# A hybrid decoder layer on one core: dense work in pinned pieces, modulation sums in an earlier stage, four borders reordered

## The chip, the cores and the metric

The kernel runs on one core of a Trainium2 chip. The metric is the device time of one execution in microseconds, the median of several; three runs of the kernel before gave 2275.9 to 2278.8, median 2276.56. TensorE (PE) multiplies, VectorE (DVE) and ScalarE (ACT) work elementwise and read the matmul banks (PSUM), GpSimd (POOL) does small powers and issues stores, SyncE (SP) issues loads. Each of them executes its queue in order.

## The reference

One layer of a post-norm decoder, sequence and width 1024, float32. It is a mixing part and a squared-ReLU MLP, each with modulation sums from a condition vector:

```python
mod = silu(c) @ w_ada + b_ada            # 6 sections of 1024: shift, scale, gate, twice
u = x * (1 + scale1) + shift1
hq, hf, hi, hg, rq, rk, rv, rg, ga, gb = split(u @ w_in)
ya = hgrn2(hq, hf, hi, hg) @ w_pa        # 8 heads of a gated linear recurrence
yb = retention(rq, rk, rv, rg, positions) @ w_pb     # 4 heads, rotary, chunks of 128
y = (sigmoid(ga) * ya + sigmoid(gb) * yb) @ w_o
x = layer_norm(alpha * x + (1 + gate1) * y)
u = x * (1 + scale2) + shift2
y = square(relu(u @ w_up + b_up)) @ w_down + b_down
out = layer_norm(alpha * x + (1 + gate2) * y)
```

HGRN: S_t = diag(f_t) S_{t-1} + k_t v_t, o_t = S_t^T q_t with k = 1 - f. Retention is the same with a fixed decay per head.

## The kernel before

**Dense products.** A float32 number is kept as a high part and a rest (`split`, L169: a copy on ACT to the high part, then a subtraction on DVE for the rest), and a product is three matmuls (`mm3`, L175 to L177) of 128x128 by 128x512. `dense_T` (L362) makes one 128x512 block with 24 of them. Larger products use a seven-product scheme (`natural`, `seven`). Weights come through one stream: pieces of 512 KB are loaded by SP into a ring of four buffers ("raw"), split, and handed out by `W` in a fixed order, some tiles ahead.

**Stages.** (1) Start: the first two modulation sections, u, its splits. (2) Input projection by `natural` (hi, rv; the rotary angles are computed beside it) and `seven` (24 "kept" groups: hg, ga, then rq, rg, rk, rg for each retention head); results go to DRAM. (3) HGRN: for each head four dense halves (q and forget gate, `h_dense`) are woven with the recurrence `h_rec` of the head before (`weave`, 4 steps against 13). (4) Retention: 4 heads of 10 steps (`r_head`: two steps of transposes and scores, eight chunks), with the HGRN branch's projection (`h_merge`, w_pa) and the 16 remaining groups of modulation sums (`ada_group`) dealt among them. (5) `merge_seven` (w_pb), (6) `out_proj` with the first norm and u for the MLP, (7) up by `seven`, (8) `down_seven` with the last norm.

**The recurrence of a head** (`h_rec`) on PE: L793 (scores inside pairs), then three levels of L831 (scores of ever larger blocks), L863 (k transposed), L874 (state updates), L890 and L894 (output), and a few steps later L917 (output transposed, in `h_out`). Between two levels DVE copies scores under masks (L799, L800, L840) and multiplies k and X by decays (L807, L821, L822, L848 to L851), which the next level reads. ACT makes sigmoids (L752 to L759), copies banks (L865, L897) and scales outputs (L903) by factors from POOL (L911).

**Retention.** `r_qk` transposes k (L1048), splits it, and `r_scores` (L1061) needs one of the two "a" banks that the split has to free. Each chunk updates the state bank G (L1113, copied by ACT at L1115) and makes an output bank (mm3 into psb, L1121, copied at L1123). `r_norm` and, four steps later, `r_out` (L1145, L1147) follow.

**What sets the order.** The program is traced in Python order; a planner then fixes each engine's queue. It works by its own estimate of when an instruction is ready, takes what is traced earlier first, and may put later work ahead of work that it takes to be waiting. `keep_in_program_order` puts an instruction behind all that was traced before it on its engine (a pin; it bounds it on one side only), `issue_after` does so for a block of instructions behind a given one, and `behind` orders two matmuls of one bank. `later(n, f)` defers f by n ticks of the recurrence.

**The modulation sums.** A group sums w_ada columns weighted by the condition: eight DVE steps of 128x256 (`ada_step`, L563 and L565), then a matmul with ones (`ada_row`, L1164, or `ada_cols`, L571), the bias, and a store or a column of `mod`. Groups of sections gate2, gate1, scale2, shift2, four each.

**Borders.** At the border to retention, `h_merge` first splits eight tiles of 128x1024 (the HGRN heads' output, loaded through the raw ring, "ohr") in one step. In `out_proj` each row of 128 is normalized one step before its transposes (L1413, in `out_second`); the last row's come after the last matmul of the stage. In `down_seven`, five products are prepared (`prepare`: splits of h and w_down) before the first is multiplied, while the last additions of `seven` (L431) are still to come.

Of the kernel before, what the change touches and what calls it, by code (L numbers as in the profile page):

```python
# [19 lines left out]
P = 128  # L20
# [34 lines left out]

PA_STEPS = [6 + (31 * i + 7) // 15 for i in range(16)]

ADA_STEPS = [4 + (32 * i + 7) // 15 for i in range(16)]
# [66 lines left out]
class Trunk:  # L125
# [43 lines left out]
    def split(self, hi, lo, src):  # L169
        self.nc.scalar.activation(hi, src, AF.Copy)  # L170
        self.nc.vector.tensor_tensor(lo, src, hi.bitcast(F32), op=ALU.subtract)  # L171
# [196 lines left out]


# [52 lines left out]
    def seven(self, groups):  # L422
# [4 lines left out]
        for g, (key, use) in enumerate(groups):  # L427

            def put(m, half, bank, kept):
                t = self.et()  # L430
                V.tensor_tensor(t, bank, kept, op=ALU.add)  # L431
                use(m, half, t, False)
# [127 lines left out]
    def ada_step(self, acc, w, k, first):  # L560
        sc = self.cond[:, k:k + 1]
        if first:
            self.nc.vector.tensor_scalar(acc, w, sc, None, op0=ALU.mult)  # L563
        else:
            self.nc.vector.scalar_tensor_tensor(acc, w, sc, acc, op0=ALU.mult, op1=ALU.add)  # L565
# [172 lines left out]
    def h_cols(self, p, what, hd):  # L738
# [9 lines left out]
        for hf in (0, 1):  # L748
            sl = slice(hf * 512, hf * 512 + 512)
            pd = self.dense_T(wh, wl, hf)  # L750
# [6 lines left out]
            else:  # L757
# [3 lines left out]
                nc.vector.tensor_tensor(s["q"][:, 0:2, hf * 256:hf * 256 + 256], pr, sr, op=ALU.mult)  # L761
# [8 lines left out]
    def h_rec(self, p, hd):  # L770
# [18 lines left out]
        for bk in range(4):  # L789
            pa = ps[bk].rearrange("p (c w b) -> p c w b", c=2, w=3)  # L790
            for c in (0, 1):
                n = 2 * bk + c
                nc.tensor.matmul(pa[:, c], k[:, n * P:(n + 1) * P], q[:, :, n * 64:(n + 1) * 64], start=True, stop=True)  # L793
# [19 lines left out]
        for ln, sz in enumerate(H_SIZES):  # L813
# [13 lines left out]
            for bk in range(4):  # L827
                for c in (0, 1):
                    n = 2 * bk + c
                    mv = X[:, :, n * P:(n + 1) * P].rearrange("p w (b r) -> p b w r", r=4 * sz)[:, :, :, sz:]  # L830
                    nc.tensor.matmul(ps[bk][:, c * 192:(c + 1) * 192].rearrange("p (b w r) -> p b w r", w=2, r=3 * sz),  # L831
                                     k[:, n * P:(n + 1) * P], mv, start=True, stop=True)
# [26 lines left out]
        for hf, tag in ((0, "b"), (1, "a")):  # L859
            pb = self.ps(tag)  # L860
            for c in range(4):
                cs = slice(hf * 512 + c * P, hf * 512 + c * P + P)
                nc.tensor.transpose(pb[:, c * P:(c + 1) * P], k[:, cs], self.ident)  # L863
# [7 lines left out]
        for hf, tag in ((0, "a"), (1, "c")):  # L871
            pu = self.ps(tag)
            for c in range(4 - hf):
                nc.tensor.matmul(pu[:, c * P:(c + 1) * P], kt[hf][:, c * P:(c + 1) * P], vn(4 * hf + c), start=True, stop=True)  # L874
# [10 lines left out]
        for hf, tag in ((0, "c"), (1, "a")):  # L885
            po = self.ps(tag)
            prev = None
            for c in range(4):
                n = 4 * hf + c
                r = l = nc.tensor.matmul(po[:, c * P:(c + 1) * P], S[hf][:, c, :], vn(n), start=True, stop=n == 0)  # L890
                if prev is not None:
                    self.behind(r, prev)
                if n > 0:
# [39 lines left out]
    def gate_proj(self, what, dst, ms):  # L933
        nc = self.nc
        for m in ms:
            wh, wl = self.W((what, m // 2, m % 2))
            for hf in (0, 1):
                pd = self.dense_T(wh, wl, hf)
# [7 lines left out]
    def h_merge(self):  # L946
        nc = self.nc
        o = []
        for e in range(KT):
# [3 lines left out]
            self.split(o[e][:, 0], o[e][:, 1], t)  # L953
        yield
# [13 lines left out]
    def rotary(self):  # L968
# [30 lines left out]
        for s in range(T // W):  # L999
            cs = slice(s * W, (s + 1) * W)  # L1000
            pi = self.rp.tile([P, W], I32, tag="rot_i", bufs=1, name=self.uid("rot"))
            nc.sync.dma_start(pi, self.i["positions"][0:1, cs].to_broadcast([P, W]))
            a, m, y, n = (self.rp.tile([P, W], F32, tag="rot_" + c, bufs=1, name=self.uid("rot")) for c in "amyn")
# [828 lines left out]
```

## Time and profile before

| | |
|---|---|
| median of 3 runs | 2276.56 us |
| profiled execution, its time | 2276.54 us |
| profiled execution, its span | 2274.7 us |
| PE busy | 2216.5 us (97%) |
| DVE busy | 1661.5 us (73%) |
| ACT busy | 969.2 us (43%) |
| POOL busy | 289.1 us (13%) |
| HBM read, written | 275.87 MB, 97.53 MB |

The span runs from the first instruction to the last; the time has a little around it. A matmul's recorded duration overlaps the next one's, so busy time on PE is close to the sum of start-to-start distances where it runs without a break. In the views, a wait is shown with the instruction whose end released it, and "x" counts instructions.

### The profile page before, as it was taken

How to read it: one execution, taken by the hardware profiler on the slowest of the kernel's cores; microseconds unless marked ns; L12 is line 12 of the kernel's file. 1: busy time of each engine (PE TensorE's matmuls, PEld its weight loads, DVE VectorE, ACT ScalarE, POOL GpSimd, SP SyncE). 2: the span in 40 equal slices, each digit the busy share in tenths (PEclk: the TensorE clock that was granted, in tenths of full speed). 3: DMA queues.
4: the chain of work that ended last, by engine and by line, in shares of the span. 5: the costliest groups of instructions: out<-in, count | busy, mean ns of one | idle time of the engine just before them, and what ended most of it. 6: DMA issues, size and time to landing. Idle time of an engine off the chain costs nothing.

```text
span 2274.7 us, 29056 instructions
## 1 busy us (share of the span) xinstructions
PE 2216.5 (97%) x10214; PEld 1824.2 (80%) x10214; DVE 1661.5 (73%) x3024; ACT 969.2 (43%) x1627; POOL 289.1 (13%) x444
## 2 busy tenths in 40 slices
PE   6999999999999999999999999999999999999997
PEld 4888888888888888888867777888888888788886
DVE  7748776467676587887776777977796665667669
ACT  4533344433333323323353333452575555643441
POOL 0111011111111100100112222112011111100001
PEclk9999999999999999999999999999999999999999
DMA  9545633332333511222387878645344444967653
GB/s 306 188 159 171 195 127 118 110 109 103 118 105 115 168 47 48 75 72 77 130 278 247 267 243 286 228 153 192 111 148 153 153 153 153 315 227 245 204 175 130
DMA packets 228563, 375.33 MB, mean 165 GB/s; under 512 B 16584, under 2 KB 126912, under 8 KB 228160
## 3 DMA queue, kind: packets, MB, share of 16 engines
q1 hardware_dynamic: 199664, 279.66, 38.7%
q0 software_dynamic: 28432, 93.35, 11.0%
q8 instruction: 80, 1.31, 0.2%
q14 instruction: 67, 0.55, 0.1%
q10 hardware_dynamic: 320, 0.45, 0.1%
HBM read 275.87 MB, written 97.53 MB: 164 GB/s over the span
## 4 chain that ended last, share of the span: by engine, by line
PE 82%; DVE 8%; issue 5%; DMA 3%; ACT 2%; POOL 1%; SPq 0%; ACTq 0%; DVEq 0%; POOLq 0%
PE psd L175 14%; PE psd L176 14%; PE psd L177 14%; PE psa L176 5%; PE psa L177 5%; PE psa L175 5%; PE psc L175 4%; PE psc L177 4%; PE psc L176 4%; PE psb L1121 2%; PE psc L1113 2%; PE psb L175 2%; PE psb L176 2%; PE psb L177 1%; PE psa L831 1%
## 5 line engine op out<-in xcount | busy, mean ns | idle before, releaser
L175 PE MATMUL psd<-U,bh 128*128 128x512 f32 x616 | 239.8, 389 | 0.0
L176 PE MATMUL psd<-U,bh 128*128 128x512 f32 x616 | 239.6, 389 | 0.0
L177 PE MATMUL psd<-U,bl 128*128 128x512 f32 x616 | 239.5, 389 | 0.0
L170 ACT ACTIVATE bh<-s 128x512 fp32r<-128x512 f32 x204 | 128.9, 633 | 249.0 <-PE psd L176 82.0
L171 DVE TENSOR_TENSOR bl<-raw,bh 128x512 fp32r<-128x512 f32 x153 | 104.6, 691 | 144.5 <-ACT bh L170 143.9
L175 PE MATMUL psd<-U,wh 128*128 128x512 f32 x504 | 203.9, 407 | 0.3 <-ACT U L170 0.3
L176 PE MATMUL psd<-U,wh 128*128 128x512 f32 x504 | 198.9, 395 | 1.0 <-DVE U L171 0.7
L177 PE MATMUL psd<-U,wl 128*128 128x512 f32 x504 | 199.7, 396 | 0.0
L171 DVE TENSOR_TENSOR bl<-s,bh 128x512 fp32r<-128x512 f32 x204 | 140.1, 687 | 65.2 <-ACT bh L170 64.8
L170 ACT ACTIVATE bh<-raw 128x512 fp32r<-128x512 f32 x153 | 96.9, 637 | 194.6 <-PE psd L176 101.9
L170 ACT ACTIVATE U<-hr 128x512 fp32r<-128x512 f32 x112 | 70.6, 630 | 155.3 <-issue 64.2
L175 PEld LDWEIGHTS psd<-U,bh 128*128 128x128 f32 x616 | 115.7, 188 | 24.3 <-ACT e L419 0.3
L176 PEld LDWEIGHTS psd<-U,bh 128*128 128x128 f32 x616 | 115.7, 188 | 24.0
L177 PEld LDWEIGHTS psd<-U,bl 128*128 128x128 f32 x616 | 115.6, 188 | 23.9
L170 ACT ACTIVATE wh<-raw 128x512 fp32r<-128x512 f32 (+1 forms) x78 | 52.7, 693 | 185.8 <-PE psd L176 138.6
L175 PE MATMUL psa<-U,bh 128*128 128x512 f32 x312 | 121.4, 389 | 0.0
L176 PE MATMUL psa<-U,bh 128*128 128x512 f32 x312 | 121.4, 389 | 0.0
L177 PE MATMUL psa<-U,bl 128*128 128x512 f32 x312 | 121.4, 389 | 0.0
L176 PEld LDWEIGHTS psd<-U,wh 128*128 128x128 f32 x504 | 95.5, 189 | 20.0 <-DVE U L171 2.8
L175 PEld LDWEIGHTS psd<-U,wh 128*128 128x128 f32 x504 | 95.0, 190 | 19.9 <-issue 2.2
L177 PEld LDWEIGHTS psd<-U,wl 128*128 128x128 f32 x504 | 95.3, 189 | 19.3
L171 DVE TENSOR_TENSOR U<-hr,U 128x512 fp32r<-128x512 f32 x112 | 77.2, 689 | 43.8 <-ACT U L170 43.7
(448 smaller groups left out, 5641.2 us busy)
## 6 DMA issues: line engine op xcount, KB each, us to landing
raw<-in_w_in SPq DMA_DIRECT2D x126, 512.0 KB, 4.2
raw<-in_w_down SPq DMA_DIRECT2D x48, 512.0 KB, 4.4
raw<-in_w_pb SPq DMA_DIRECT2D x36, 512.0 KB, 4.8
raw<-in_w_ada SPq DMA_DIRECT2D x32, 512.0 KB, 5.2
raw<-in_w_up SPq DMA_DIRECT2D x32, 512.0 KB, 3.8
adw<-in_w_ada SPq DMA_DIRECT2D x16, 512.0 KB, 7.7
rv_d<-e POOLq DMA_DIRECT2D x32, 256.0 KB, 3.1
rg_d<-e POOLq DMA_DIRECT2D x32, 256.0 KB, 2.3
```

What stands on the lines that cost most here:

```text
L170: self.nc.scalar.activation(hi, src, AF.Copy)
L171: self.nc.vector.tensor_tensor(lo, src, hi.bitcast(F32), op=ALU.subtract)
L175: r = mm(out, wh, uh, start=start, stop=False, skip_group_check=more)
L176: mm(out, wh, ul, start=False, stop=False, skip_group_check=more)
L177: return r, mm(out, wl, uh, start=False, stop=stop, skip_group_check=more)
L831: nc.tensor.matmul(ps[bk][:, c * 192:(c + 1) * 192].rearrange("p (b w r) -> p b w r", w=2, r=3 * sz), k[:, n * P:(n + 1) * P], mv, start=T ...
L1113: mm(G[e], l[:, n % 2, es], r, start=n == 0 and i == 0, stop=i == 2, skip_group_check=n > 0)
L1121: mm(po, st["q"][:, e, n * P:(n + 1) * P], gs[e], start=False, stop=e == 1)
```

## The change

Five things are changed.

1. HGRN's dense halves and the later gb gates yield after every six matmuls (`pieces_T`), so that they are dealt out in pieces: `H_FILL` gives the number of pieces after each of a head's 13 steps, and the dense work runs four pieces (one half) further ahead than by whole heads (`H_LEAD`). The first matmul of each group of the recurrence, and the product of q and its sigmoid on DVE, are pinned. The remaining gate pieces fill the tail of the last head and the two score steps of the first retention head, six to one.
2. The 16 groups of modulation sums leave the retention stage and its weight ring and run in the input projection beside the kept groups that aren't rq or rk (`ada_rest`): 64 parts of 256 KB with two buffers of their own, the first of each part's two steps pinned, and the end of a group two parts later, on bank "b". The rotary steps now all lie beside `natural`, in a pool that is closed before the sums' pool opens.
3. Merge: `h_merge` splits two tiles per step, pinned on ACT and DVE, in retention steps 2 to 5.
4. Last row: half of the plain up product (its first 24 matmuls) is traced before the flush that makes the last row's transposes, which are pinned behind it; the "relu" tiles become four.
5. Down: the fourth and fifth preparation stand behind the last addition of `seven` on DVE (`issue_after`).

Beside these, "ot" in the retention stage has three buffers in place of two.

```diff
+H_FILL = (0, 4, 3, 0, 3, 0, 2, 0, 1, 0, 2, 0, 1)
+H_LEAD = 4
...
-    def split(self, hi, lo, src):
-        self.nc.scalar.activation(hi, src, AF.Copy)
-        self.nc.vector.tensor_tensor(lo, src, hi.bitcast(F32), op=ALU.subtract)
+    def split(self, hi, lo, src, pin=lambda r: r):
+        pin(self.nc.scalar.activation(hi, src, AF.Copy))
+        pin(self.nc.vector.tensor_tensor(lo, src, hi.bitcast(F32), op=ALU.subtract))
...
+    def pieces_T(self, wh, wl, half):
+        pd = self.ps("d")
+        for k in range(KT):
+            uh, ul = self.ublk(k, half)
+            self.mm3(pd, wh[:, k], wl[:, k], uh, ul, k == 0, k == KT - 1)
+            if k in (1, 3, 5):
+                yield
+        return pd
...
-                V.tensor_tensor(t, bank, kept, op=ALU.add)
+                self.last_sum = V.tensor_tensor(t, bank, kept, op=ALU.add)
...
-            pd = self.dense_T(wh, wl, hf)
+            pd = yield from self.pieces_T(wh, wl, hf)
...
-                nc.vector.tensor_tensor(s["q"][:, 0:2, hf * 256:hf * 256 + 256], pr, sr, op=ALU.mult)
+                self.tc.keep_in_program_order(
+                    nc.vector.tensor_tensor(s["q"][:, 0:2, hf * 256:hf * 256 + 256], pr, sr, op=ALU.mult))
...
-                nc.tensor.matmul(pa[:, c], k[:, n * P:(n + 1) * P], q[:, :, n * 64:(n + 1) * 64], start=True, stop=True)
+                r = nc.tensor.matmul(pa[:, c], k[:, n * P:(n + 1) * P], q[:, :, n * 64:(n + 1) * 64], start=True, stop=True)
+                if n == 0:
+                    self.tc.keep_in_program_order(r)
...
-            self.split(o[e][:, 0], o[e][:, 1], t)
-        yield
+            self.split(o[e][:, 0], o[e][:, 1], t, self.tc.keep_in_program_order)
+            if e % 2:
+                yield
...
-        ot = self.rt("ot", (P, 4, P), 2)
+        ot = self.rt("ot", (P, 4, P), 3)
...
+    def ada_rest(self):
+        ap = self.aw
+        parts = [(s, g, q) for s, g in ADA_ORDER for q in range(4)]
...
+        for n, (s, g, q) in enumerate(parts):
+            if q == 0:
+                acc = ap.tile([P, 256], F32, tag="adacc", bufs=2, name=self.uid("acc"))
+            w = loaded.pop(n)
+            for j in (0, 1):
+                r = self.ada_step(acc, w[:, j], 2 * q + j, q + j == 0)
+                if j == 0:
+                    self.tc.keep_in_program_order(r)
+            if n + 2 < len(parts):
+                load(n + 2)
+            if q == 1 and ends is not None:
+                ends()
...
-        self.tick(True)
-        drain(self.u2)
...
+                r = nc.tensor.transpose(pt[:, k * P:(k + 1) * P], z[:, (4 * q + k) * P:(4 * q + k + 1) * P], self.ident)
+                if t == 7 and k == 0:
+                    self.tc.keep_in_program_order(r)
...
-        for n in range(AHEAD):
+        for n in range(3):
             prepare(n)
+        with self.tc.issue_after(self.last_sum.ins):
+            for n in range(3, AHEAD):
+                prepare(n)
...
-            for _ in k.seven([(key, use) for key, _, use in kept]):
-                next(rotary, None)
+            k.aw = k.pool("ada", "left", se)
+            ada = k.ada_rest()
+            for n, _ in enumerate(k.seven([(key, use) for key, _, use in kept])):
+                if n // 3 < len(kept) and kept[n // 3][0][0] not in ("rq", "rk"):
+                    next(ada, None)
+                    if n % 3 == 2:
+                        next(ada, None)
+            drain(ada)
...
-        drain(k.h_dense(0))
         gb = k.gate_proj("gb", k.gb_d, range(4, KT))
+        fill = chain(*(k.h_dense(h) for h in range(HH)), gb)
+        for _ in range(16 + H_LEAD):
+            next(fill)
         for h in range(HH):
-            if h + 1 < HH:
-                weave(k.h_dense(h + 1), k.h_head_rec(h), 4, 13)
-            else:
-                weave((next(gb) for _ in range(4)), k.h_head_rec(h), 4, 18)
+            rec = k.h_head_rec(h)
+            for n in H_FILL:
+                next(rec)
+                for _ in range(n):
+                    next(fill)
+            for _ in rec:
+                next(fill)
...
-            weave(gb, (next(heads) for _ in (0, 1)), 4, 2)
-            next(merge)
+            weave(fill, (next(heads) for _ in (0, 1)), 6, 1)
             for n in range(2, 10 * RH):
+                if n < 6:
+                    next(merge)
                 next(heads)
-                if n in ADA_STEPS:
-                    k.ada_group(*ADA_ORDER[ADA_STEPS.index(n)])
...
             k.out_proj(first)
+            plain = k.up_plain()
+            next(plain)
+            k.tick(True)
+            drain(k.u2)
```

The same pin stands on the first matmul of each bank group in L831 (per level), L863, L874 and L890.

More of the change, by code (lines that the diff above doesn't have):

```diff
@@ L1145, in r_out, with load @@
             nc.tensor.transpose(pb[:, e * P:(e + 1) * P], of[:, e * P:(e + 1) * P], self.ident)
-        ot = self.rt("ot", (P, 4, P), 2)
+        ot = self.rt("ot", (P, 4, P), 3)
         nc.vector.tensor_tensor(ot, pb.rearrange("p (e t) -> p e t", e=4), rg, op=ALU.mult)
         nc.gpsimd.dma_start(self.or_d[h].rearrange("(e p) t -> p e t", p=P)[:, :, n * P:(n + 1) * P], ot)
-    def ada_group(self, sec, g):
-        raws = self.W(("ada", sec, g))
-        acc = self.rp.tile([P, 256], F32, tag="adacc", bufs=2, name=self.uid("acc"))
-        for k in range(KT):
-            self.ada_step(acc, raws[k // 4][:, k % 4, :], k, k == 0)
+    def ada_rest(self):
+        ap = self.aw
+        parts = [(s, g, q) for s, g in ADA_ORDER for q in range(4)]
+        loaded = {}
+        def load(n):
+            s, g, q = parts[n]
+            c0 = s * D + 256 * g
+            t = loaded[n] = ap.tile([P, 2, 256], F32, tag="adw", bufs=2, name=self.uid("adw"))
+            self.nc.sync.dma_start(t, self.i["w_ada"][256 * q:256 * q + 256, c0:c0 + 256].rearrange("(k p) c -> p k c", p=P))
+        load(0)
+        load(1)
+        yield
+        ends = None
+        for n, (s, g, q) in enumerate(parts):
[5 more added lines that the diff above has]
+                if j == 0:
+                    self.tc.keep_in_program_order(r)
+            if n + 2 < len(parts):
+                load(n + 2)
+            if q == 1 and ends is not None:
+                ends()
+            if q == 3:
+                ends = lambda acc=acc, s=s, g=g: self.ada_end(acc, s, g)
+            yield
+        ends()
@@ L1477, in up_plain @@
                 use(m, half, self.dense_T(*wt[m], half), True)
+                if (half, m) == (0, 0):
+                    yield
     def down_seven(self):
@@ L1718, in build @@
             k.sin = k.rp.tile([P, T], F32, name="sin")
-            rotary = k.rotary()
-            for n, _ in enumerate(chain(*(k.natural(key, put) for key, _, put in wide))):
-                if n >= 28 and n % 4 == 1:
-                    next(rotary)
-            for _ in k.seven([(key, use) for key, _, use in kept]):
-                next(rotary, None)
+            with ExitStack() as st:
+                k.rt_p = k.pool("rotparts", "left", st)
+                rotary = k.rotary()
+                for n, _ in enumerate(chain(*(k.natural(key, put) for key, _, put in wide))):
+                    if n >= 20 and n % 4 == 1:
+                        next(rotary)
+                drain(rotary)
+            k.aw = k.pool("ada", "left", se)
[6 more added lines that the diff above has]
+            drain(ada)
     k.hst = {}
```

50 lines of the change are left out of this document (25 added, 25 removed).

## The prediction

> **What bounds the kernel now.** I read the page first, then the waits of the TensorE queue, then the timeline around each long wait.
>
> ```profile
> core 0: 2274.7 us, clock 0.997
> ```
>
> ```profile
> PE 2216.5 (97%) x10214; PEld 1824.2 (80%) x10214; DVE 1661.5 (73%) x3024; ACT 969.2 (43%) x1627; POOL 289.1 (13%) x444
> ```
>
> TensorE (PE) bounds everything: of the span only 2274.7 - 2216.5 = 58 us pass without a matmul. No matmul is removed, so what can be won is idle time. The waits of PE between 780 and 1970 us:
>
> ```profile
> PE psa L831 <- DVE k L807: 10.4, 7, 1.8
> PE psa L1061 <- DVE U L171: 6.7, 3, 3.6
> PE psb L175 <- ACT U L1123: 2.4, 2, 1.2
> PE psd L175 <- DVE e L431: 2.1, 1, 2.1
> PE psa L1413 <- ACT z L1391: 2.0, 2, 1.1
> PE psc L1113 <- ACT g L1115: 0.8, 1, 0.8
> PE psa L831 <- DVE U L822: 0.7, 1, 0.7
> PE psa L1145 <- DVE ot L1147: 0.3, 1, 0.3
> PE psa L1048 <- DVE ot L1147: 0.3, 1, 0.3
> ```
>
> Columns: total, times, longest, in us. Together 25.7 us; the other 32 lie at the start and the end, which the diff doesn't touch. L831 waits once in each of the eight HGRN heads; L1061 (the retention scores) three times; L175, L1113, L1145 and L1048 sit in the retention stage; L1413 at the output projection (one of its two waits is the last row of the stage, 1.1); psd L175 at the start of down. These are the places that the diff names. One HGRN head, PE:
>
> ```profile
> 834.71 0.39 PE L176 MATMUL psd<-U,wh 128*128 128x512 f32 x1
> 834.94 0.39 PE L177 MATMUL psd<-U,wl 128*128 128x512 f32 x1
> 835.16 1.46 PE L793 MATMUL psa<-hq,k 128*128 128x192 f32 x8
> 836.46 1.46 PE L793 MATMUL psc<-hq,k 128*128 128x192 f32 x8
> 837.76 0.60 PE L917 MATMUL psb<-cst,ob 128*128 128x128 f32 x4
> ...
> 838.66 0.40 PE L177 MATMUL psd<-U,wl 128*128 128x512 f32 x1
> 840.67 1.57 PE L831 MATMUL psa<-U,k 128*128 128x192 f32 x8 [1.61 <-DVE k L807]
> ...
> 848.62 1.46 PE L831 MATMUL psa<-U,k 128*128 128x192 f32 x8
> ```
>
> A dense matmul is recorded with 0.39 but the next starts 0.227 later: 0.16 of each record overlaps the next, so a wait costs its idle time and 0.16 more. A record of L793 (and L831, same shape) takes 1.30/8 = 0.162; the four transposes of L917 0.44. Between L793 and the first L831 stand only three dense matmuls (the last at 838.66), and DVE is not done by then:
>
> ```profile
> 837.05 0.69 DVE L761 TENSOR_TENSOR hq<-psd,sg 128x512 f32<-128x512 f32 x1 [2.06 <-ACT sg L759]
> ...
> 839.89 0.72 DVE L807 TENSOR_TENSOR k<-k,f 128x512 f32<-128x512 f32 x1
> ```
>
> DVE stood 2.06 us in front of L761, a product of the next head that needs a sigmoid, with the work that L831 needs queued behind it.
>
> **HGRN in pieces.** Same matmuls; each 24-matmul half becomes four pieces of six (6 x 0.227 = 1.36 us), placed by H_FILL, and the first matmul of every recurrence group is pinned behind them. Four pieces (5.45 us) now lie between L793 and the first L831. From L793's end (837.76) to L807's end (840.61) DVE needed 2.85 us with the 2.06 stall, which is covered; L761 is pinned later on DVE. Removed: 11.1 us of waits and 8 x 0.16 = 1.3, so **12.4**.
>
> What is late next? The last product before the second and the third L831 group is L822 (durations, then first and last start):
>
> ```profile
> L822 DVE TENSOR_TENSOR U<-U,D x2: 681/687/693, 847.2 to 854.5; 128x512 f32<-128x512 f32 x2
> ```
>
> The second L831 group had 848.62 - 840.67 = 7.95 us from the first; now it has 16 x 0.162 + 0.44 + 18 x 0.227 = 7.12. The first L822 ends at 847.9, 7.2 after the first group began: late by 0.1, and by 0.6 more if L761, now pinned near there, goes ahead of it. The third has 2.6 + 4.09 = 6.68, and its L822 ended 855.2 - 848.62 = 6.6 after: no wait, 0.5 if a weight split falls in between. Then the transposes:
>
> ```profile
> 859.49 0.60 ACT L752 ACTIVATE f<-psd 128x512 f32<-128x512 f32 x1 [9.26 <-PE psd L177]
> ...
> 861.78 0.59 ACT L865 ACTIVATE kt<-psb 128x512 f32<-128x512 f32 x1
> ```
>
> Four gate activations (2.3 us) precede the copy L865. The new order ends a forget-gate half right before the transposes, so kt can be ready 0.2 + 2.3 + 0.6 = 3.1 us after it, while PE gets there after 0.87 + 1.36 = 2.2: up to 0.9 late, 0 if the planner (which may still pull unpinned dense matmuls ahead) fills it. New waits per head: 0 to 2.1. I take 0.3, near the lower end, since both L822 rows come out within 0.1 of enough: 2.4 in all. Net **-10.0** (0 to 2.1 x 8 = 17 against 12.4: from -12.4 to +4.4).
>
> **Modulation sums.** 16 groups of eight DVE steps leave the retention stage for the second half of the input stage (hg, ga and rg groups); 32 loads of 512 KB become 64 of 256 KB, no longer in the ring of four "raw" buffers.
>
> ```profile
> L565 DVE SCALAR_TENSOR_TENSOR acc<-raw,small,acc 128x256 f32<-128x256 f32 x112 | 52.6, 483 | 1.6
> ```
>
> ```profile
> 520.00:558.00 38.00, 38.00 (x170) 31.46 (x169) 27.89 (x45) 14.27 (x24) 4.33 (x8) 1.00 0.33 112
> ```
>
> The second row is a window of one rotated group (which gets no sums) and one rg: after its length PE, weight loads, DVE, ACT, POOL, clock, DMA share. DVE has 27.9 of 38 and gets 8 x 0.48 = 3.9: 84%. The DMA engines are a third busy. PE sits at 38.00 of 38.00; what hides the sums are the weight blocks split ahead of it. On SP the 64 loads stand in order among the w_in loads, and each waits until DVE has freed one of two buffers: behind a late one wait the next w_in pieces, and behind a pinned sum whose load is late wait the additions that free PE's banks. A group's four parts lie 19/4 = 4.8 us apart, so two loads ahead give 9 us for a landing (the 512 KB merge loads below took 6.3). I take 0, up to +3. The closing matmuls, eight bias rows on SP and eight small stores on POOL (4.3 of 38 busy) move along at the same cost; the two rotary steps that lay beside the first kept groups move back into the stage before, where PE doesn't wait either.
>
> The retention stage loses 16 x 8 x 0.48 = 61 us of DVE, but DVE load is not what made PE wait there:
>
> ```profile
> 1271.84 0.63 ACT L170 ACTIVATE wh<-raw 128x512 fp32r<-128x512 f32 x1 [5.48 <-DMA raw<-in_w_pa]
> ```
>
> ```profile
> 1273.85 2.05 PE L1061 MATMUL psa<-U,U 128*128 128x128 f32 x16 [2.85 <-DVE U L171]
> ```
>
> ACT stood 5.48 us on a weight split whose load had not landed, with the copy that the scores need behind it in order. Of the four raw buffers the sums held two at a time; without them w_pa is loaded a group ahead. So 2.85 goes, and likewise 2.4 (psb) and 0.6 ("ot" has three buffers now): with restarts 5.9 + 5 x 0.16 = 6.7; I take **-6.0** (-6.7 to -3).
>
> **Scores and merge.** The longest wait of L1061 is where the retention stage begins:
>
> ```profile
> 1144.44 2.05 PE L1061 MATMUL psa<-U,U 128*128 128x128 f32 x16 [3.64 <-DVE U L171]
> ```
>
> ```profile
> L170 ACT ACTIVATE U<-ohr x8: 1057/1060/1067, 1140.2 to 1152.6; 128x1024 fp32r<-128x1024 f32 x8
> L171 DVE TENSOR_TENSOR U<-ohr,U x8: 1216/1224/1226, 1141.3 to 1153.7; 128x1024 fp32r<-128x1024 f32 x8
> ```
>
> ```profile
> ohr<-oh_d SPq DMA_DIRECT2D x8, 512.0 KB, 6.3
> ```
>
> A third, 6.7 - 3.64 - 2.85 = 0.2, precedes it. The eight merge splits ran ahead of the second scores' splits. Now they are pinned behind and dealt two at a time over four retention steps, so 0.2 + 3.6 + 0.8 (L1113) and restarts, 5.2, go. But their work (8 x 1.06 ACT, 8 x 1.22 DVE) stands among those steps, and a slot of the ring turns over in 6.3 + 1.06 + 1.22 = 8.6 us; with w_pa prefetched into two of four slots, eight tiles take four rounds, 34 us. An ACT queue that waits on a landing holds the copies that the recurrence needs. New waits 0 to 10; I take 4: **-1.2** (-5.2 to +5).
>
> [...] The 16 matmuls behind the 3.64 us wait took 2.05, as did those behind 2.85: no restart price beyond 0.16. [...]
>
> **Last row and down.** The first 24 up matmuls (5.45 us) now precede the last row's transposes, which lacked 1.1: **-1.3** with the restart. Behind them one more dense group covers the splits that follow. At down, two of five preparations go behind the last sum on DVE:
>
> ```profile
> 1960.55 0.69 DVE L431 TENSOR_TENSOR e<-psd,e 128x512 f32<-128x512 f32 x1
> ```
>
> Four splits of 0.6 (pitch) earlier, this sum ends 2.4 earlier, more than the 2.1 wait; the two preparations are needed three products (8 us) later. **-2.0** (-2.2 to -1).
>
> Sum: -10.0 - 6.0 - 1.2 - 1.3 - 2.0 = -20.5. The profiled execution took 2276.54 (1.8 outside its span), like the median 2276.56: **2256.0 us**.
>
> **The rivals.** (1) Pinned transposes wait in HGRN. L917 now follows L793 after six dense matmuls:
>
> ```profile
> 869.64 0.59 ACT L897 ACTIVATE ob<-psc 128x512 f32<-128x512 f32 x1
> ...
> 875.43 2.45 ACT L903 ACTIVATE ob<-ob,rs 128x128 f32<-128x128 f32 x8 [3.01 <-POOL rs L911]
> ```
>
> From L897 to the first half's four L903 (875.43 + 1.3) is 7.1 us; PE gets there after what is left of the second output bank (16 records of 0.11, the pitch of a transpose, so 1.7, less some 0.6 before L897 starts), one piece and L793: 1.1 + 1.36 + 2.6 = 5.0. If the planner misjudges this by 2.1, as it misjudged L807 by 1.6, that is 8 x 2.1 = 17 instead of 2.4: 2270.5. Against: any of the 24 unpinned matmuls can go ahead.
> (2) The merge ring binds with 10 us: 2262.
> (3) Slower: the DVE chain between L831 groups becomes the bound. If L921, L761 and two weight splits (4 x 0.6 = 2.4) all fall inside it at both inner levels, each head waits 2 x 2.4 + 0.1 = 4.9, 39 in all, against 12.4 + 10.5 won: 2276.5 + 16 = 2293. It decides from 22.9/8 = 2.9 us per head. Against: the rows above have one L921 inside a level and still fit.
> (4) The change doesn't do what it says: the planner draws dense work off ahead of the pinned groups, so HGRN's waits only move (0), w_pa is helped by half (-3), the ring binds (+4.8): 0 - 3 + 4.8 - 1.3 - 2.0 = -1.5, 2275.
> [...]
>
> **Chances.** Forecast 0.60; (1) 0.14; (2) 0.12; (3) 0.07; (4) 0.07. About 0.2% (4.6 us) can be told from no change: faster is below 2272. Faster 0.60 + 0.12 + 0.10 of (1) = 0.82; same 0.04 + 0.07 = 0.11; slower 0.07. Low end: everything that can go, 12.4 + 6.7 + 5.2 + 1.3 + 2.2 = 27.8, is 2248.8; high end at (1) with some margin: 2249 to 2272.
>
> **What would show it.** Right: L831 <- L807 gone from the waits, under 3 us left in HGRN; no ACT wait of microseconds on w_pa; L1061 waiting under 2 us in all; no L1413 wait at the last row; no psd wait on L431; PE still at 38.00 of 38.00 beside the sums. Wrong: new PE waits named L831 <- L822 or U, L874 <- kt, L917 <- ob, or a retention wait on g (L1115) behind a landing of ohr.

## The result and the profile after

The kernel after takes **2257.3 us** (median of 5 runs, 2256.0 to 2258.9), the kernel before 2276.56 (5 runs, 2275.5 to 2278.8): ratio **0.9911, 95% interval 0.9900 to 0.9922**, 0.9% faster, where 2256.0 (2249 to 2272) was predicted. Its profiled execution has a span of 2256.5 us, 18.2 less than before. That the sum came out right doesn't mean that its terms did, and several of them didn't.

Line numbers move in the kernel after: mm3 is L177 to L179 (before L175 to L177), the splits L172 and L173, the HGRN scores L805 and L845 (L793, L831) with the products in front of them L821, L835 and L836 (L807, L821, L822), the transposed output L939 (L917), retention's scores L1084 (L1061), the additions of `seven` L443 (L431). In experiments they can differ by a few more.

The cores and the busy times of the page after, and all waits of PE between 60 and 2262 us (total, times, longest):

```profile
core 0: 2256.5 us, clock 0.997
```

```profile
PE 2215.7 (98%) x10214; PEld 1822.1 (81%) x10214; DVE 1660.4 (74%) x3024; ACT 967.3 (43%) x1625; POOL 282.1 (13%) x444
```

```profile
PE psd L178 <- DVE U L173: 2.5, 4, 0.8
PE psd L177 <- DVE e L443: 2.4, 4, 0.7
PE psd L178 <- DVE stat L1157: 1.4, 1, 1.4
PE psa L1463 <- ACT z L1443: 0.9, 1, 0.9
PE psa L1168 <- DVE ot L1170: 0.3, 1, 0.3
PE psd L177 <- ACT mv L172: 0.2, 1, 0.2
```

Of the 25.7 us shown before, HGRN's and those of the retention scores are gone. 7.7 are left, and most of it is new: three waits of 0.5 to 0.7 on L443 beside the modulation sums (the fourth is the one at down, 2.1 before and 0.5 now), three on `U` of L173 where the merge splits are dealt out (the fourth, 0.7, stands behind the last row), and 1.4 at the first merge product.

The stages, each from the first matmul that is its own to the first of the next (the starts of these records in the two traces):

| stage | before | after | difference | what else moved |
|---|---|---|---|---|
| kept groups, modulation sums, the first dense halves of HGRN | 484.16 | 496.95 | +12.8 | 16 closing matmul groups come in: 9.5 |
| HGRN | 327.87 | 320.53 | -7.3 | 24 dense matmuls more: 5.45 |
| retention | 270.84 | 248.01 | -22.8 | the closings leave: 9.85; 24 dense matmuls fewer: 5.45 |
| merge | 154.17 | 155.37 | +1.2 | |
| output projection | 118.53 | 118.27 | -0.3 | |
| up | 285.77 | 286.21 | +0.4 | |
| down | 321.79 | 318.65 | -3.1 | |

The start and `natural` are 0.9 longer (312.53 against 311.60). The diff moves two rotary steps there, but three more runs of this same program, below, took 311.0 to 312.1, so nothing can be told. A closing is costed by the distance from the matmul in front of it to the dense matmul behind it, less one pitch, and 0.10 for the slow second matmul behind that. With the moved work taken out, HGRN won 7.35 + 5.45 = 12.8 and the retention stage 22.8 - 9.85 - 5.45 = 7.5; the input stage lost 12.8 - 9.5 = 3.3.

HGRN is the plainest. On PE, the start of the head that follows the one shown in the prediction (its first row of L793), then one whole head after, from one first row of L805 to the next, with the score groups between them:

```profile
876.33 1.46 PE L793 MATMUL psa<-hq,k 128*128 128x192 f32 x8
```

```profile
887.11 1.46 PE L805 MATMUL psa<-hq,k 128*128 128x192 f32 x8
...
889.71 0.60 PE L939 MATMUL psb<-cst,ob 128*128 128x128 f32 x4
...
895.62 1.46 PE L845 MATMUL psa<-U,k 128*128 128x192 f32 x8
...
903.91 1.47 PE L845 MATMUL psa<-U,k 128*128 128x192 f32 x8
...
926.28 1.46 PE L805 MATMUL psa<-hq,k 128*128 128x192 f32 x8
```

A head took 876.33 - 835.16 = 41.17 and takes 926.28 - 887.11 = 39.17. Its 220 matmuls at their usual pitches (96 of 0.227, 64 of 0.162, 60 of 0.11) need 38.8, so next to nothing is left to win. What DVE does in the meantime:

```profile
888.30 0.68 DVE L773 TENSOR_TENSOR hq<-psd,sg 128x512 f32<-128x512 f32 x1
...
890.57 0.73 DVE L821 TENSOR_TENSOR k<-k,f 128x512 f32<-128x512 f32 x1
891.22 0.68 DVE L836 TENSOR_TENSOR U<-U,D 128x512 f32<-128x512 f32 x1
...
903.02 0.67 DVE L836 TENSOR_TENSOR U<-U,D 128x512 f32<-128x512 f32 x1
```

The q product (L773) has no stall in front of it now, and the last product before the first L845 ends at 891.90, 3.7 us early. The one before the second group ends at 903.69, and that group starts at 903.91: 0.2 us is all there is.

The new waits of the input stage begin on DVE:

```profile
504.97 0.69 DVE L223 TENSOR_TENSOR s<-raw,raw 128x512 f32<-128x512 f32 x1 [3.58 <-DMA raw<-in_w_in]
505.58 0.68 DVE L443 TENSOR_TENSOR e<-psa,e 128x512 f32<-128x512 f32 x1
506.18 0.68 DVE L173 TENSOR_TENSOR bl<-s,bh 128x512 fp32r<-128x512 f32 x1
506.78 0.69 DVE L223 TENSOR_TENSOR s<-s,raw 128x512 f32<-128x512 f32 x1
507.38 0.68 DVE L707 TENSOR_TENSOR e<-e,e 128x512 f32<-128x512 f32 x1
507.98 0.35 DVE L575 TENSOR_SCALAR acc<-adw,small 128x256 f32<-128x256 f32 x1
508.24 0.69 DVE L443 TENSOR_TENSOR e<-psd,e 128x512 f32<-128x512 f32 x1
```

DVE stood 3.58 us for pieces of w_in; the addition that frees PE's bank came at 508.24, behind what had queued up and behind a pinned sum (L575). DVE's waits for w_in from 300 to 780 us before, and to 790 after:

```profile
DVE s L221 <- DMA raw<-in_w_in: 19.3, 20, 1.8
```

```profile
DVE s L223 <- DMA raw<-in_w_in: 44.3, 22, 3.6
```

### The profile page after: what moved, and what is told of

Same layout as the page of the kernel before. It is cut to its first block, busy times and chain, and to the rows that moved or that the text cites. A ratio compares the mean times of both kernels' runs of the same rounds, so it can differ in the third digit from the quotient of the medians.

```text
span 2256.5 us, 29106 instructions
## 1 busy us (share of the span) xinstructions
PE 2215.7 (98%) x10214; PEld 1822.1 (81%) x10214; DVE 1660.4 (74%) x3024; ACT 967.3 (43%) x1625; POOL 282.1 (13%) x444
## 5 line engine op out<-in xcount | busy, mean ns | idle before, releaser
L177 PE MATMUL psd<-U,bh 128*128 128x512 f32 x616 | 241.9, 393 | 1.8 <-DVE e L443 1.8
L179 PE MATMUL psd<-U,bl 128*128 128x512 f32 x616 | 239.8, 389 | 0.0
L172 ACT ACTIVATE bh<-s 128x512 fp32r<-128x512 f32 x204 | 128.6, 631 | 239.7 <-PE psd L178 78.9
L177 PE MATMUL psd<-U,wh 128*128 128x512 f32 x504 | 202.4, 405 | 0.4 <-ACT U L172 0.4
L179 PE MATMUL psd<-U,wl 128*128 128x512 f32 x504 | 201.8, 400 | 0.0
L172 ACT ACTIVATE bh<-raw 128x512 fp32r<-128x512 f32 x153 | 97.1, 638 | 206.1 <-PE psd L178 100.4
L173 DVE TENSOR_TENSOR bl<-raw,bh 128x512 fp32r<-128x512 f32 x153 | 104.5, 689 | 105.8 <-ACT bh L172 92.9
L173 DVE TENSOR_TENSOR bl<-s,bh 128x512 fp32r<-128x512 f32 x204 | 139.5, 685 | 49.4 <-ACT bh L172 49.3
L177 PEld LDWEIGHTS psd<-U,bh 128*128 128x128 f32 x616 | 115.6, 188 | 31.0 <-issue 3.5
L172 ACT ACTIVATE U<-hr 128x512 fp32r<-128x512 f32 x112 | 70.5, 630 | 151.0 <-issue 56.7
L179 PEld LDWEIGHTS psd<-U,bl 128*128 128x128 f32 x616 | 115.7, 188 | 24.2
L172 ACT ACTIVATE wh<-raw 128x512 fp32r<-128x512 f32 (+1 forms) x78 | 52.7, 695 | 173.8 <-PE psd L178 136.2
L177 PE MATMUL psa<-U,bh 128*128 128x512 f32 x312 | 121.4, 389 | 0.0
L179 PE MATMUL psa<-U,bl 128*128 128x512 f32 x312 | 121.4, 389 | 0.0
L177 PEld LDWEIGHTS psd<-U,wh 128*128 128x128 f32 x504 | 95.1, 190 | 19.1 <-ACT U L172 2.3
L179 PEld LDWEIGHTS psd<-U,wl 128*128 128x128 f32 x504 | 95.3, 189 | 18.7
L173 DVE TENSOR_TENSOR U<-hr,U 128x512 fp32r<-128x512 f32 x112 | 76.7, 685 | 44.7 <-ACT U L172 44.5
```

What stands on the lines that cost most here:

```text
L172: pin(self.nc.scalar.activation(hi, src, AF.Copy))
L173: pin(self.nc.vector.tensor_tensor(lo, src, hi.bitcast(F32), op=ALU.subtract))
L177: r = mm(out, wh, uh, start=start, stop=False, skip_group_check=more)
L179: return r, mm(out, wl, uh, start=False, stop=stop, skip_group_check=more)
```

## The experiments

Every ratio is to the kernel before, timed beside the experiment; its medians there were 2278.0 to 2279.0, 1.5 to 2.4 above the first result, so ratios are compared, and stages of the traces.

### The HGRN part alone

```diff
 (the kernel before, and)
+H_FILL = (0, 4, 3, 0, 3, 0, 2, 0, 1, 0, 2, 0, 1)
+H_LEAD = 4
+            pd = yield from self.pieces_T(wh, wl, hf)
+            weave(fill, (next(heads) for _ in (0, 1)), 6, 1)
             next(merge)
```

> The kernel before with the HGRN part alone (pieces, fills, pins of the group heads and of the q product). The forecast's step: 12.4 us of waits go, 0.3 a head comes back, so 10.0 less than before, 2266.6. The reading of the two traces: a head's period goes from 41.15 to 39.17 us (2.0 less, not 1.25), the first head's from 39.40 to 38.45, so 0.95 + 7 x 2.0 = 15 less, 2261.6. Rival (the waits only move): the retention stage begins with its dense work further drawn off and gives a part back; over 2268.

Measured: 2270.39, ratio **0.9963 (0.9950 to 0.9976)**, span 8.1 under before. The rival comes nearest. HGRN itself did what it does in the kernel after (head periods 39.2 us, the stage 12.3 us shorter with the 24 matmuls counted), but the retention stage took 270.78 with 24 dense matmuls fewer, so it lost 5.4. Its score waits in this kernel:

```profile
PE psa L1086 <- DVE U L175: 6.8, 3, 2.7
```

That is the 6.7 of before again, though in three waits of 2.1, 2.1 and 2.7 instead of 0.2, 3.6 and 2.9, so it explains none of the 5.4. Windows of PE around two of them (window, then busy time of PE, weight load, DVE, ACT and POOL, the granted clock, the DMA share):

```profile
1128.60:1132.01 3.41, 1.35 (x7) 0.78 (x5) 2.18 (x5) 2.12 (x4) 0.00 (x0) 1.00 1.06 400
1132.01:1135.42 3.41, 3.41 (x17) 3.41 (x17) 2.65 (x4) 2.93 (x4) 0.00 (x0) 0.50 0.79 311
...
1183.20:1186.62 3.42, 1.34 (x9) 0.82 (x7) 1.05 (x4) 1.93 (x4) 0.73 (x1) 1.00 0.81 244
1186.62:1190.03 3.41, 3.41 (x17) 3.41 (x17) 1.86 (x6) 1.34 (x3) 0.56 (x1) 0.50 0.95 234
```

```profile
1186.59 3.68 PE L1086 MATMUL psa<-U,U 128*128 128x128 f32 x16 [2.08 <-DVE U L175]
```

Behind each of two waits of 2.1 us the clock was 0.50 for 3.41 us, and the 16 score matmuls took 3.68 us instead of 2.05. Each costs 1.7 more than the wait, half of the 3.41. The two together are 3.4 of the 5.4. DVE's own load isn't what holds these scores up: just before them it stands idle for 1.2, 2.4 and 2.9 us until ACT has split, and ACT waits for w_pa.

### The modulation sums alone

```diff
 (the kernel before, and ada_rest with its pool, the rotary steps, and)
-        ot = self.rt("ot", (P, 4, P), 2)
+        ot = self.rt("ot", (P, 4, P), 3)
-                if n in ADA_STEPS:
-                    k.ada_group(*ADA_ORDER[ADA_STEPS.index(n)])
```

> The kernel before with the modulation sums alone moved to the input stage (their loads, the rotary steps and the third ot buffer with them). The forecast's step: nothing lost in the input stage, 6.0 won in the retention stage: 2270.6. The reading of the trace: three waits psd <- e (0.83 + 0.76 + 0.71) appear beside the sums, so 6.0 - 2.3 = 3.7 won, 2272.9. Rival: the retention waits come from the score splits on DVE and not from w_pa, they stay, and only the 2.3 is left: 2279.

Measured: 2276.6, ratio **0.9992 (0.9982 to 1.0002)**: nothing that can be told from no change. The input stage grew by 13.9, of which the closings are 9.65, so 4.3 are lost there; the retention stage lost 15.5 us, 9.85 of it the closings, so 5.7 are won; the merge lost 1.2. ACT's wait on w_pa from 1130 to 1400 us, which was 10.6 us before, is gone in this kernel; the one on the merge's tiles has grown from 5.4 to 12.7 (before, then here):

```profile
ACT wh L170 <- DMA raw<-in_w_pa: 10.6, 6, 5.5
```

```profile
ACT U L168 <- DMA ohr<-oh_d: 12.7, 5, 4.2
```

So the cause of the score waits was named rightly, but the eight merge splits, still at one place, then wait for their own landings, and behind a PE wait of 2.1 us that follows them the clock is halved again (0.50 from 1173.23 on, for 3.41 us). The ring itself shows in SP's waits of the kernel before from 1120 to 1400 us: each of the eight loads of w_pa there was held until a modulation sum had freed its buffer. In the kernel after, none was.

```profile
SPq L313 <- DVE acc L565: 46.9, 26, 3.4
```

### All but the modulation sums

```diff
 (the kernel after, with ada_group, its weights in the stream and ADA_STEPS as before)
+                if n in ADA_STEPS:
+                    k.ada_group(*ADA_ORDER[ADA_STEPS.index(n)])
```

> The kernel after with the modulation sums in the retention stage and their loads in the ring of four again; pieces, dealt merge splits and both late borders stay. Theory 1 (what holds the scores up is the ring, which the sums' loads share with w_pa): ACT waits on w_pa of over 5 us are back, 10.6 to 13.3 in all as in the two kernels that have the sums there, and with them score waits of about 2.8 and 1.2 and 1.2; the closing matmuls and the three waits beside the sums move with them, so 6 to 8 more than after, about 2264. Theory 2 (the eight merge splits at one place hold the scores up): dealing them out was enough, 2259. Theory 3, rival (2) of the forecast (the ring binds once dealt splits and sums share it): 10 more, 2267 or above.

Measured: 2263.84, ratio **0.9937 (0.9923 to 0.9950)**. Theory 1, also in its row:

```profile
ACT wh L174 <- DMA raw<-in_w_pa: 13.5, 6, 4.9
```

As long as the sums take half of the ring, dealing the splits out leaves score waits of 3.0 and 1.0 us, and the clock is halved twice, once for 6.83 us; the retention stage takes 268.09, 2.7 less than in pieces_only. Against the ratio of the kernel after, moving the sums is worth 0.0026 here, 5.9 us, and 0.0008 alone, 1.8. With intervals of 0.0010 to 0.0014 on each ratio these two aren't clearly apart; that the parts need each other rests on the waits and windows of the traces.

### The merge splits at one place

```diff
 (the kernel after, and)
-            self.split(o[e][:, 0], o[e][:, 1], t, self.tc.keep_in_program_order)
-            if e % 2:
-                yield
+            self.split(o[e][:, 0], o[e][:, 1], t)
+        yield
...
             weave(fill, (next(heads) for _ in (0, 1)), 6, 1)
+            next(merge)
```

> The kernel after with the eight merge splits at one place again, unpinned, ahead of the retention steps. The forecast's step: 1.2 won by dealing them out, so 2258.5 without it. The reading of the trace: the dealt splits still cost 2.6 (0.47 + 0.93 + 0.93 + 0.25 on psd <- U<-ohr), the old place cost 3.64 + 0.2 + 0.8 and restarts: 2.6 more, 2260. [...] Rival (2), the ring binds in the dealt order: 4.8 less than after, 2252.5.

Measured: 2259.34, ratio 0.9916 (0.9904 to 0.9928). Not told apart: the retention stage is 249.08 against 248.01, and the runs below show that the same program gives 247.5 to 249.3. The 3.64 us wait of before doesn't come back (1.5 at most in this kernel), so what such a wait costs wasn't tested here.

### The last row and down as before

```diff
 (the kernel after, and)
             k.out_proj(first)
-            plain = k.up_plain()
-            next(plain)
...
-        for n in range(3):
+        for n in range(AHEAD):
             prepare(n)
-        with self.tc.issue_after(self.last_sum.ins):
```

> The kernel after with the last row and down as before (the first up product behind the drained u2 parts, all five down preparations ahead). The forecast's steps: 1.3 + 2.0 more, 2260.6. The reading of the trace: down won 3.2 (landmarks at its start and at the end -15.1 and -18.2), the last row nothing net (its 1.1 wait is gone, a new one of 0.73 on the splits of u stands 10 us later): 3.2 more at down, 0.4 at the last row, 2260.9. Rival (both waits only move on): 2257.3.

Measured: 2258.75, ratio 0.9912 (0.9899 to 0.9925); by time nothing is told. By the profile down takes 322.84 instead of 318.7 to 319.1, about 4 more, and the output projection 117.4, no more than with the change (117.1 to 118.3). The profiled execution was the slowest of its five, 2262.59; the others took 2256.9 to 2259.6. Why down costs 4 and not 2 shows in its windows, and in those of the kernel before:

```profile
1944.48:1947.90 3.42, 0.85 (x5) 0.48 (x3) 3.42 (x7) 2.90 (x6) 1.62 (x3) 1.00 0.99 329
1947.90:1951.31 3.41, 3.41 (x10) 2.67 (x9) 3.41 (x6) 1.81 (x5) 1.08 (x2) 0.50 1.02 386
```

```profile
1958.49:1961.90 3.41, 1.34 (x7) 0.80 (x6) 3.41 (x7) 2.77 (x6) 1.62 (x3) 1.00 0.95 323
1961.90:1965.31 3.41, 3.41 (x10) 2.63 (x9) 3.41 (x6) 2.01 (x5) 1.08 (x2) 0.50 1.03 395
```

So behind the wait at down, 2.57 us here and 2.07 in the kernel before, the clock was halved too, 0.50 for 3.41 us, which is another 1.7. Not every wait at this border was followed by that: pieces_only has one of 1.98 us, but there, in windows of 3.41 us counted on from its halving at 1132.01, the edge between two windows falls into the wait, the first window keeps 1.62 us busy, the clock stays at 1.00, and down takes 320.10, 1.7 less than in the kernel before:

```profile
1951.21:1954.62 3.41, 1.62 (x8) 1.00 (x6) 3.41 (x6) 2.95 (x6) 1.25 (x3) 1.00 1.05 380
1954.62:1958.03 3.41, 3.22 (x14) 2.69 (x15) 3.41 (x7) 3.11 (x6) 1.45 (x3) 1.00 0.96 365
```

### Three kernels that are one

```diff
 (a piece less between the first and the second L845 group)
-H_FILL = (0, 4, 3, 0, 3, 0, 2, 0, 1, 0, 2, 0, 1)
+H_FILL = (0, 4, 2, 0, 4, 0, 2, 0, 1, 0, 2, 0, 1)
```

> The kernel after with one of the three pieces between the first and the second L845 group moved behind the second. In the trace of after the last product before the second group (L836) ends 0.2 us before that group begins, in six heads alike. Theory 1, rival (3) of the forecast (the DVE chain between the groups is the next bound): a wait of 1.36 - 0.2 = 1.15 and 0.16 of restart in each of eight heads, 10.5 more, 2267.8, and head periods of 40.5 instead of 39.17. Theory 2 (the planner pulls unpinned dense matmuls forward and fills the hole): no change, 2257.3, head periods 39.2.

```diff
 (no pins on PE in HGRN: at L805, L845, L879, L892 and L910)
-                if n == 0:
-                    self.tc.keep_in_program_order(r)
```

> The kernel after without the pins on the first matmuls of the HGRN groups (L805, L845, L879, L892, L910); the pieces, their places and the pin of the q product stay. Theory 1 (the pieces do it, the planner keeps to their places): no change, head periods 39.2, 2257.3. Theory 2, rival (4) of the forecast (the planner draws dense work ahead of the unpinned groups, as before): waits of 1.5 come back in front of the first L845 group, head periods 40.7 to 41.2, 12 to 16 more, 2270.

```diff
 (weights of the sums loaded one part ahead)
         load(0)
-        load(1)
...
+            if n + 1 < len(parts):
+                load(n + 1)
             w = loaded.pop(n)
...
-            if n + 2 < len(parts):
-                load(n + 2)
```

> The kernel after with the loads of the modulation weights issued one part ahead of the sums instead of two, so that the SP queue waits for the sum before the last one and no longer for the last one. Theory 1 (SP stands 346 us in 61 of these loads and sends the w_in loads behind them late; DVE then stands 44 instead of 19 us before the sums of weight blocks, and its additions reach PE late three times): the three waits of 0.8 go, 2.3 less, 2255.0. Theory 2 (the lead was needed: the 256 KB now land behind the pinned sum): DVE waits on adw grow from 3.6 to over 20 us, and PE waits more, 2260 or above. Theory 3 (the w_in loads are late by traffic, not by the queue): no change, 2257.3.

Measured: 2258.25 (0.9911, 0.9897 to 0.9924), 2258.4 (0.9914, 0.9901 to 0.9928) and 2259.61 (0.9916, 0.9903 to 0.9930). In the traces the instructions of PE, DVE and ACT stand in the same order as in the kernel after, row for row: the planner made one program of all four. For the first two that is the answer, theory 2 of less_cover and theory 1 of no_pins: neither the pins on PE nor the exact place of the third piece has any effect here, since the planner puts 23 dense matmuls between the first and the second group, whether 18 or 12 are traced there. For the third it means that nothing was tested; SP's wait for the sums is the same 346 us. The four also show how far one program differs from run to run: medians 2257.3 to 2259.6, and stages by up to 1.8 us in retention and 2.2 in the input stage.

### One piece in front of the first L845 group

```diff
-H_FILL = (0, 4, 3, 0, 3, 0, 2, 0, 1, 0, 2, 0, 1)
+H_FILL = (0, 1, 3, 0, 3, 0, 2, 0, 4, 0, 2, 0, 1)
```

> The kernel after with one piece instead of four between L805 and the first L845 group in each HGRN head, three moved behind the transposes; in the compiled order 6 dense matmuls stand there, 24 in after, 3 in the kernel before. Theory 1 (the cover is what removed the wait, and DVE now needs 2.2 us from the end of L805 to the end of L836, as in the trace of after): PE arrives 0.44 + 1.36 = 1.8 after L805, a wait of 0.4 and 0.16 of restart a head, 4.5 more, 2262, head periods 39.7. Theory 2 (the forecast's: without cover the 2.06 stall before the q product is back too): 2.85 needed plus what is queued, 1.0 to 1.2 a head, 9 more, 2267, periods 40.3. Theory 3 (the place of the pieces doesn't matter, any dense matmul between the groups does): 2258, periods 39.2.

Measured: 2266.29, ratio **0.9946 (0.9934 to 0.9959)**, head periods 930.10 - 889.87 = 40.2. The wait on L836 comes back once in each head, of the size that theory 1 gave, while the time is the one of theory 2:

```profile
889.87 1.46 PE L805 MATMUL psa<-hq,k 128*128 128x192 f32 x8
...
894.83 1.54 PE L845 MATMUL psa<-U,k 128*128 128x192 f32 x8 [0.36 <-DVE U L836]
896.33 1.54 PE L845 MATMUL psc<-U,k 128*128 128x192 f32 x8
...
930.10 1.46 PE L805 MATMUL psa<-hq,k 128*128 128x192 f32 x8
```

```profile
PE psa L845 <- DVE U L836: 3.0, 8, 0.7
```

The head lost twice as much, about 1.0 against 0.53: the second half of the group (bank c) also starts 0.2 late (1.50 behind the first half, which takes 1.30), and the second group, cut in two, takes 0.24 more than at the usual pitches (906.23 - 902.26 = 3.97 instead of 3.73). So the cover removes the wait, but not alone. The stall in front of the q product isn't back (0.7 us in two in this kernel and in after, 15.9 in nine before), so theory 2's cause isn't there. Without it DVE needs 2.2 us from the end of L805 (to 894.67) where it needed 2.85 before, so by the two traces about 0.65 of each wait of 1.6 went with the stall and the rest with the matmuls in between. For 2.2, two pieces, 0.44 + 2.7, would be enough; that wasn't run.

### The loads of the sums on POOL's queue

```diff
-            self.nc.sync.dma_start(t, self.i["w_ada"][256 * q:256 * q + 256, c0:c0 + 256].rearrange("(k p) c -> p k c", p=P))
+            self.nc.gpsimd.dma_start(t, self.i["w_ada"][256 * q:256 * q + 256, c0:c0 + 256].rearrange("(k p) c -> p k c", p=P))
```

> The kernel after with the 64 loads of the modulation weights issued on POOL's queue instead of SP's; the orders of PE and ACT are those of after. Theory 1 (the waits of SP for the sums, 346 us in 61, send the w_in loads behind them late): SP loses these waits, DVE stands under 25 us before the sums of weight blocks instead of 44, PE's waits psd <- e beside the sums go (2.3 of the 2.4 to 4.5), 2.5 less, 2255. Theory 2 (POOL now waits for the sums and the stores of the kept gates stand behind, so the e tiles come free late): new PE waits of 1 us a group on e, 2265. Theory 3 (the w_in loads are late by the traffic): no change, 2257 to 2259.

Measured: 2264.99, ratio **0.9940 (0.9928 to 0.9953)**, slower than after. Theory 1 is refuted. SP's waits for the sums went, and SP now stands as long for buffers of the ring (SP's queue from 300 to 790 us, after and then here); w_in comes later for DVE, not earlier (last row, here):

```profile
SPq L1184 <- DVE acc L576: 345.7, 61, 18.3
```

```profile
SPq L315 <- DVE bl L173: 364.2, 41, 19.7
```

```profile
DVE s L223 <- DMA raw<-in_w_in: 55.9, 21, 4.6
```

Theory 2 gives the time, but its waits on e are only 4.3 us in six, not one a group. The edit also moves the loads to another kind of queue (from 480 to 780 us q0, software_dynamic, moves 23.6 MB instead of 16.0), so it isn't a test of the order on SP alone. The input stage is 500.8, 1.6 above the highest of the others. The output projection takes 120.0; PE waits 2.7 us there for a normalized row (L1463), 0.9 in after, for a cause that stays open.

### The w_pa products two steps later, alone and with POOL's queue

```diff
-PA_STEPS = [6 + (31 * i + 7) // 15 for i in range(16)]
+PA_STEPS = [8 + (29 * i + 7) // 15 for i in range(16)]
```

> The kernel after with the sixteen w_pa products of the merge beginning two retention steps later (step 8 instead of 6). Theory 1, rival (2) of the forecast at a small price (the dealt splits reach the dense matmuls of w_pa late, 0.47 + 0.93 + 0.93 + 0.25 of PE waits psd <- U from 1149 to 1177 us): these go, 2.6 less, 2255. Theory 2 (fewer steps are left for the products, and the first merge product waits longer for the norm at the end): the 1.6 there grows to 3 or more, 2257 to 2259.

> Both of the last two edits in the kernel after. If both theories 1 hold the two gains lie in different stages and add up: 5 less than after, 2252 to 2254. If one of them only moves its wait on, no better than the better of the two alone.

Measured: 2256.18, ratio 0.9900 (0.9885 to 0.9915), and with the other queue 2260.56, 0.9918 (0.9905 to 0.9932). Of the waits on the dealt splits 0.3 is left in the retention stage (1.8 in after), and a new 0.9 on psb stands beside it:

```profile
PE psd L178 <- DVE mv L173: 0.9, 1, 0.9
PE psb L177 <- ACT U L1146: 0.9, 1, 0.9
PE psa L1168 <- DVE ot L1170: 0.3, 1, 0.3
PE psd L178 <- DVE U L173: 0.3, 1, 0.3
```

The stage takes 246.39, and 246.65 with the other queue, against 247.5 to 249.3 in the four runs of one program, so 1 to 3 are won there; the interval of the time holds after's ratio too. This is the best kernel of the study, by a hair, and the two edits didn't add up since the other is a loss.

## Why the prediction was right, and where it wasn't

**HGRN, -10.0 predicted, -12.8 by the trace.** The mechanism holds: L831 <- L807 is gone, cover_one brings a wait back at the same group (on L836, the product behind L821), and the q product no longer stalls. The 12.4 that was to go is right: from the last dense matmul to a score group PE lost 12.5 us in all before, and 0.06 after. Two terms were off. Another 1.8 before, 0.1 after, stood in front of the state updates (L874), 0.2 to 0.3 a head, which the wait view doesn't list. And of the new waits, 0.3 a head or 2.4 in all, 1.3 came, all in the last head: its two groups of output transposes (L939) take 1.28 and 1.21 instead of 0.60, one matmul at a time behind the scaling of `ob` (L925). In front of the second score group nothing came back, since the planner moved five dense matmuls more than the 18 that I counted there. The reserve is 0.2 us, as thin as I had it.

**Modulation sums in the input stage, 0 predicted (to +3), +3.3 measured**, and 3.8 to 5.5 in the eight other kernels that have DVE's order there, so the 3.3 is the luckiest of nine. This is the step that failed: "I take 0, up to +3". PE isn't busy throughout: it waits three times with a named release, 2.3 with the restarts, and the rest lies in smaller pieces. The prediction named the way ("behind a late one wait the next w_in pieces") and priced it at nothing because DVE was 84% busy on average. The chain is late w_in pieces, then a burst of six queued DVE instructions with a pinned sum among them. What makes w_in late stays open: taking the sums' loads off SP's queue made it worse, but put them on another kind of queue; the DMA traffic, whose share rose from 0.34 to 0.44 between 330 and 780 us, wasn't tested by itself.

**Retention, -6.0, and the scores and merge border, -1.2; together -7.5 in the stage, and +1.2 behind it.** That the waits came from the ring that w_pa shares with the sums is shown twice (sums_only without them, sums_in_ring with them), and by SP's waits for the sums. The dealt splits cost less than the 4 taken: 1.8 in waits. But 1.4 of the gain came back at a place that I had not looked at, the first merge product, which waits for the norm of the last chunk. How much the dealing is worth by itself isn't settled: 1 us, no more than a repetition.

**The last row, -1.3 predicted, -0.3 measured.** The wait is gone, as predicted, but the stage's other wait of its kind, 0.9, is as it was, 0.7 on a split of u is new, and with the old order the stage is no longer.

**Down, -2.0 predicted (at most 2.2), -3.1 measured.** The wait on L431 was 2.1 and is 0.5 now; the rest is the clock. I wrote that a wait has "no restart price beyond 0.16" after two places where the matmuls behind a long wait ran at full speed. That was the wrong step: at down, the third place, the window behind the wait ran at 0.50. In pieces_only this 1.7 wasn't paid (the clock at 1.00, down 320.10 against 321.79 before); the 1.5 of the wait alone is less than the 2.0.

**The clock.** Between start and end each halving lasts 3.41 us, one 6.83 (sums_in_ring), and the two in pieces_only start 1186.62 - 1132.01 = 54.61 us apart, 16 times 3.413. So I read the traces in windows of 3.41 us, counted from a halving. PE wasn't idle in those in front of the halvings: they had 0.83 to 1.44 of 3.41 us busy, one even 1.88. Counted in the same way from the halving at 1961.90, the 3.64 us wait before falls in two windows,

```profile
1139.29:1142.71 3.42, 1.51 (x7) 0.90 (x5) 1.37 (x2) 2.29 (x3) 0.00 (x0) 1.00 0.69 253
1142.71:1146.12 3.41, 1.68 (x15) 1.68 (x16) 3.41 (x5) 3.23 (x6) 0.54 (x1) 1.00 0.68 213
```

1.51 and 1.68 us busy and both at 1.00, so the longer wait cost no clock and the one of 2.07 did. I took the price of a wait from this one and the one of 2.85; what the clock did bears on down, and on what the parts are worth alone.

**The rivals.** (1) happened in the last head alone, at 1.3 us instead of 17: L939 waits there in pieces too small for a row in the waits. (2), the ring, is there at 1.8 instead of 10. (3) is refuted for this change by the planner's five matmuls, though cover_one shows how near such a bound lies. (4) is refuted for the whole, and describes pieces_only well: there the waits did move.

**Why the sum was near.** Beside the steps lie -2.8 (HGRN), +3.3 (sums), -0.4 (the closings are a little cheaper in their new place), -0.3 and +1.2 (retention and first merge product), +1.0 (last row), -1.1 (down) and +1.4 at the start and in up, for which the forecast had no term: +2.3, and -20.5 + 2.3 is the -18.2 of the spans. Errors of both signs, as large as the gains of the small steps, cancelled. That the sum came within 1.3 us of the median is luck to that extent.

## What to carry to other kernels

Here a TensorE wait of 2.07 us cost 1.7 us more through the clock and one of 3.64 us nothing more, so read the granted clock around every long wait before you give it a price, not around one or two; the wait at down, 2.07 us in one trace and 1.98 in another, paid the 1.7 in the first alone. Parts of a change that share a ring or a stage are not additive: alone, the pieces gave 0.4% and the sums 0.1%, and dealing the splits or the two late borders, taken out of the whole, changed it by under 0.1% each; yet the whole gave 0.9%. And where a planner fixes the order, compare the orders of two kernels before you time them, since pins and places that look different can be the same program.

## What the runs showed of the hardware

In the traces of before and of pieces_only the halvings of TensorE's granted clock lie whole windows apart: in before, the one at down starts at 1961.90 and one at the start of the kernel at 36.79, each with 0.50 for 3.41 us, 564.0 windows of 3.4133 us from one to the other; in pieces_only, the two above, 16 windows. In four runs of one program (after, less_cover, no_pins, sums_one_ahead) that first halving starts 36.13 to 37.98 us into the span (37.86 in after), so the windows don't begin at one distance from the kernel's start. From there to 2240 us, windows with 0.83 to 1.44 us busy stand in eight places of five traces, and each was followed by a clock of 0.50; those with 1.51, 1.62 and 1.68 above weren't, nor twelve with 1.64 to 1.81 in HGRN (before, sums_only). One with 1.88 (seven 128x512 matmuls, borders_old) was, so the recorded busy share alone doesn't tell the two apart (the second half of the 6.83 us in sums_in_ring stands behind 2.41 us busy, but that window itself ran at 0.50):

```profile
1169.66:1173.07 3.41, 1.88 (x7) 1.04 (x7) 3.41 (x5) 1.40 (x2) 0.00 (x0) 1.00 0.62 223
1173.07:1176.48 3.41, 3.41 (x10) 2.62 (x9) 0.73 (x3) 0.99 (x2) 1.35 (x2) 0.50 0.84 244
```

A closing sum in a run of dense matmuls costs 0.72 us with its two 128x256 matmuls and 0.46 with its four of 128x1 (in after, the slow second matmul behind it included), 9.5 for the 16; behind transposes, before, nearly the same, 9.85.
